# Loading the first activations through ScalarE's DMA queue instead of SyncE's in a two-layer decoder trunk

## The chip, the cores and the metric

The kernel runs on one core of a Trainium2 chip. The metric is the device time of one execution in microseconds (us). The program before was timed three times: median 2251.39 us, lowest 2250.98, highest 2251.55. A separate execution was recorded by the hardware profiler, and all durations in this document come from such recordings.

The engines are TensorE (PE, its weight loads PEld), VectorE (DVE), ScalarE (ACT), GpSimd (POOL) and SyncE (SP). SP and ACT can issue DMA transfers. Each of the two has a queue of its own, and the transfers of both run on the same 16 DMA engines. In the profile SP's queue is q1 and ACT's is q10.

## The reference

The reference is a decoder trunk of two layers for 256 tokens of width 2048, in float32.

```python
for l in range(DEPTH):                      # DEPTH = 2
    h = _rmsnorm(x, attn_norm[l])
    z = jnp.einsum('bsd,de->bse', h, w_in[l])          # 2048 -> 4934
    ...                                     # three kinds of attention on parts of z
    x = x + jnp.einsum('bsm,md->bsd', mix, w_o[l])
    h = _rmsnorm(x, ffn_norm[l])
    x = x + _conv_gated_mlp(h, ffn_w_up[l], ffn_conv_w[l], ffn_conv_b[l], ffn_w_down[l])
return _rmsnorm(x, final_norm)
```

Only the start matters here: the first RMS norm of the input x, and the first columns of the input projection w_in of layer 0.

## The kernel before, in words

All weights of both layers are laid out on the host as one stream of 128x128 blocks in the order of use. The kernel walks this stream once. A chunk is 16 blocks, a raw tile of 128x2048 float32 (1024 KB), and three raw tiles rotate (`load`, L109 to L115; the pool has bufs=3). Every chunk is converted in pieces: ACT casts it to a rounded `hi` (L140), DVE subtracts to get the rest, `lo` (L141). Five `hi` and five `lo` tiles rotate. Each product then takes matmuls with `hi` and with `lo`.

The input x arrives twice. Transposed, as eight tiles `xg` of 256 KB (two slices of 128 features each), it feeds the first norm and the first projection; in its natural layout, as two tiles `xr` of 1024 KB (L589), it is needed only for the residual much later. `Norm.split` multiplies a slice of x by the norm's gain on ACT (L396) and takes the rest on DVE (L397), giving the 16 tiles `h`. The row scale 1/rms isn't needed for these products. It is applied when a result is drained from PSUM, so its computation runs beside the first projection: eight squares of the `xg` tiles on ACT (L547), a running sum on DVE (L549), a column sum on PE (`misc`, L361), a square root on ACT with its table load (L365), a reciprocal and two scalings on DVE (L366, L369), and a second PE step that spreads the result over the rows (L376). Three PSUM banks take the first three results; the fourth block of the projection goes to the bank `s`. The next one (the tile `mm_531` in the order below) needs one of the three banks back, and that drain needs the row scale.

`load_first` (L117 to L126) issues the first three chunks in quarters of 256 KB, and between the first eight quarters the eight `xg` tiles. Before it, ACT issues the 42 columns of `par` that hold the norm's gains (21 KB) and computes one Square on a tiny tile (L277), which brings a table load. Eleven matmuls on a zeroed tile (L274) run on PE meanwhile. After `load_first` SP issues a table of constants (`cs`), the positions (`pint`) and the rest of `par`.

A scheduler orders the instructions of each engine from the program text and its own estimates; within an engine they run in that order. Each DMA signals its landing on one of eight counters, DMAHW0 to DMAHW7, which are handed out in turn; a transfer that takes a counter again waits, on the engine that issues it, until the counter's earlier transfer has landed.

Of the kernel before, what the change touches and what calls it, by code (L numbers as in the profile page):

```python
# [12 lines left out]
AF = mybir.ActivationFunctionType  # L13
# [20 lines left out]
Q_AN, Q_FN, Q_QN, Q_KN, Q_DG, Q_FB, Q_CV = 0, 16, 32, 36, 40, 41, 42  # L34
# [33 lines left out]
def kernel(ctx: ExitStack, tc: tile.TileContext, xin, xnat, pos, wstream, cst, par, fin, out):  # L68
    nc = tc.nc
# [10 lines left out]
    def nm(s):  # L80
        uid[0] += 1
        return f"{s}_{uid[0]}"

    def slot(dtype=F32):
        return slots.tile([P, 2 * T], dtype, tag="slot", name=nm("slot"))

    def tmp():
        return work.tile([P, T], F32, tag="tmp", name=nm("tmp"), bufs=15)

    def small(n):  # L90
        return work.tile([P, n], F32, tag="small", name=nm("small"), bufs=15)
# [7 lines left out]
    def f(ap):  # L99
        return ap.bitcast(F32)  # L100
# [16 lines left out]
    def load_first():  # L117
        for c in range(3):
            t = wpool.tile([P, CH * P], F32, tag="raw", name=nm("raw"), bufs=3)
            src = wflat[c * CH * P * P : (c + 1) * CH * P * P].rearrange("(p e) -> p e", p=P)  # L120
            for i in range(4):
                a = slice(i * 4 * P, (i + 1) * 4 * P)
                nc.sync.dma_start(t[:, a], src[:, a])
                if c < 2:
                    nc.sync.dma_start(xg[4 * c + i], xin[4 * c + i])
            raws[c] = t  # L126

    def convert(s, between=None):
# [135 lines left out]
    pr = [const.tile([P, Q_W], F32, tag=f"par{l}", name=f"par{l}") for l in range(DEPTH)]  # L264
# [3 lines left out]
    xg = [slot().rearrange("p (j t) -> p j t", j=2) for k in range(KT // 2)]  # L268
# [5 lines left out]
        nc.tensor.matmul(hot, heat[:, :P], heat, start=(i == 0), stop=(i == 10))  # L274
    warm = small(4)
    nc.vector.memset(warm, 0.0)
    nc.scalar.activation(warm, warm, AF.Square)  # L277
    nc.scalar.dma_start(pr[0][:, :Q_CV], par[0, :, :Q_CV])
    load_first()
    nc.sync.dma_start(cs, cst)  # L280
    nc.sync.dma_start(pint, pos)
# [284 lines left out]
    for l in range(DEPTH):  # L566
# [48 lines left out]
        for j in range(2):  # L615
            c = f(c_hi[fo, j * T : (j + 1) * T])
# [26 lines left out]
        for j in range(2):  # L643
            for h in range(H_FOX):
                if j == 0:
                    fqk.append(slot())
                i = j * H_FOX + h + 1
# [87 lines left out]
        for qo in (Q_KN, Q_QN):  # L735
            ln = Norm(q_[:, qo : qo + 4], 512)
            tiles = []
            for k in range(4):
                u = total(mm_t(hx))
                c = tmp()  # L740
# [263 lines left out]
```

## Time and profile before

| | us |
|---|---|
| median of 3 runs | 2251.39 |
| profiled execution | 2251.53 |
| its span, first to last instruction | 2249.8 |
| PE busy | 2236.4 |
| ACT busy | 1204.2 |
| DVE busy | 1487.6 |
| first weight cast on ACT starts | 5.09 |
| first matmul of the projection starts | 6.91 |

Times inside the execution count from the first instruction. The profiled execution takes 1.73 us more than its span, and 0.14 us more than the median of the runs. A row of the timeline gives start and duration, the engine, the source line, the operation, and what it writes and reads; "x2" means that two instructions are merged in it. A row of the issues gives the number of transfers, the size of one, and the median time from issue to landing.

### The profile page before, as it was taken

Reading aid. Unit: us, or ns where it says so; the run is one execution under the profiler, and the core shown is the slowest. Engines: PE = TensorE matmul, PEld = TensorE weight load, DVE = VectorE, ACT = ScalarE, POOL = GpSimd, SP = SyncE. Lnnn points to the kernel's source line nnn. Section 1 sums busy time; section 2 is a strip of 40 time slices with the busy share of each in tenths; the row PEclk is TensorE's granted clock in tenths of the full one; section 3 lists DMA queues with packets and bytes.
Section 4 is the critical chain, followed back from the end, with each engine's and each line's share of the span. In section 5 each row is a group of like instructions: output and inputs, shape, how many; then the busy total and the mean of one; then the engine's idle time right before and its main releaser. Section 6 shows DMA issues by size and latency. Waiting matters only on the chain.

```text
span 2249.8 us, 31033 instructions
## 1 busy us (share of the span) xinstructions
PE 2236.4 (99%) x12083; PEld 1929.6 (86%) x12083; DVE 1487.6 (66%) x2317; ACT 1204.2 (54%) x1867; POOL 404.7 (18%) x395
## 2 busy tenths in 40 slices
PE   9999999999999999999999999999999999999998
PEld 8888978888888888888888889788888888888886
DVE  8767766677764577775574787566666546777653
ACT  7455645555543455554454565455555435555543
POOL 4600000222210022210050110003333101222210
PEclk9999999999999999999999999999999999999999
DMA  8544445455555555555555444355555555555653
GB/s 314 200 160 159 156 141 181 162 194 194 187 206 189 186 189 187 190 202 188 187 182 193 150 167 159 131 185 178 186 185 185 207 200 187 188 187 187 208 201 114
DMA packets 60915, 413.59 MB, mean 184 GB/s; under 512 B 6880, under 2 KB 7008, under 8 KB 11744
## 3 DMA queue, kind: packets, MB, share of 16 engines
q1 hardware_dynamic: 60048, 410.54, 51.6%
q8 instruction: 95, 1.56, 0.3%
q10 hardware_dynamic: 720, 1.07, 0.1%
q14 instruction: 52, 0.43, 0.1%
HBM read 409.49 MB, written 2.10 MB: 183 GB/s over the span
## 4 chain that ended last, share of the span: by engine, by line
PE 98%; ACT 1%; DVE 0%; DMA 0%; issue 0%; DVEq 0%; SPq 0%; ACTq 0%
PE mm L195 37%; PE mm L200 19%; PE mm L249 12%; PE mm L250 12%; PE mm L251 12%; PE s L473 2%; PE mm L234 1%; PE mm L766 1%; PE mm L767 1%; PE mm L768 1%; PE pv L505 1%; PE mm L232 1%; PE s L432 0%; PE misc L376 0%; PE pv L506 0%; ACT hi L140 0%
## 5 line engine op out<-in xcount | busy, mean ns | idle before, releaser
L141 DVE TENSOR_TENSOR lo<-raw,hi 128x1024 fp32r<-128x1024 f32 (+1 forms) x776 | 974.9, 1264 | 499.4 <-ACT hi L140 461.0
L140 ACT CAST hi<-raw 128x1024 fp32r<-128x1024 f32 (+1 forms) x776 | 800.5, 1039 | 475.7 <-PE mm L251 367.1
L195 PE MATMUL mm<-h,hi 128*128 128x512 f32 x3584 | 863.8, 392 | 0.0
L195 PEld LDWEIGHTS mm<-h,hi 128*128 128x128 f32 x3584 | 664.7, 188 | 135.6 <-ACT tmp L259 1.3
L200 PEld LDWEIGHTS mm<-h,lo 128*128 128x128 f32 x3584 | 460.6, 190 | 13.6
L200 PE MATMUL mm<-h,lo 128*128 128x256 f32 x3584 | 465.4, 283 | 0.0
L249 PE MATMUL mm<-hi,slot 128*128 128x512 f32 x992 | 387.7, 391 | 0.0
L251 PE MATMUL mm<-hi,slot 128*128 128x512 f32 x992 | 384.8, 388 | 0.0
L250 PE MATMUL mm<-lo,slot 128*128 128x512 f32 x992 | 384.7, 388 | 0.0
L824 POOL TENSOR_TENSOR tmp<-tmp,rstd 128x256 f32<-128x256 f32 x176 | 193.4, 1099 | 1037.7 <-DVE tmp L261 727.7
L827 ACT ACTIVATE tmp<-tmp,par 128x256 f32<-128x256 f32 x176 | 106.0, 602 | 312.1 <-POOL tmp L824 312.1
L249 PEld LDWEIGHTS mm<-hi,slot 128*128 128x128 f32 x992 | 186.3, 188 | 41.5 <-issue 4.0
L251 PEld LDWEIGHTS mm<-hi,slot 128*128 128x128 f32 x992 | 186.2, 188 | 38.2
L250 PEld LDWEIGHTS mm<-lo,slot 128*128 128x128 f32 x992 | 186.3, 188 | 36.8
L828 DVE SCALAR_TENSOR_TENSOR tmp<-tmp,par,tmp 128x255 f32<-128x255 f32 x176 | 84.5, 480 | 150.7 <-ACT tmp L827 150.7
L259 ACT COPY tmp<-mm 128x256 f32<-128x256 f32 (+1 forms) x233 | 85.9, 369 | 62.1 <-PE mm L195 34.1
L832 POOL TENSOR_TENSOR tmp<-tmp,tmp 128x256 f32<-128x256 f32 x88 | 75.6, 859 | 211.6 <-ACT tmp L831 209.3
L261 DVE TENSOR_TENSOR tmp<-mm,tmp 128x256 f32<-128x256 f32 (+1 forms) x233 | 97.4, 418 | 5.5 <-ACT tmp L259 5.3
L829 DVE SCALAR_TENSOR_TENSOR tmp<-tmp,par,tmp 128x254 f32<-128x254 f32 x176 | 85.0, 483 | 6.2
L831 ACT ACTIVATE tmp<-tmp 128x256 f32<-128x256 f32 x88 | 36.8, 418 | 61.8 <-DVE tmp L829 61.7
L249 PE MATMUL mm<-hi,h 128*128 128x512 f32 (+1 forms) x192 | 68.3, 356 | 0.0
L251 PE MATMUL mm<-hi,h 128*128 128x512 f32 (+1 forms) x192 | 67.9, 354 | 0.0
(193 smaller groups left out, 1470.9 us busy)
## 6 DMA issues: line engine op xcount, KB each, us to landing
raw<-in_w SPq DMA_DIRECT2D x381, 1024.0 KB, 4.8
raw<-in_w SPq DMA_DIRECT2D x14, 256.0 KB, 5.3
slot<-in_x SPq DMA_DIRECT2D x8, 256.0 KB, 5.2
x<-in_xn SPq DMA_DIRECT2D x2, 1024.0 KB, 10.7
slot<-in_fin SPq DMA_DIRECT2D x4, 256.0 KB, 6.2
out<-x SPq DMA_DIRECT2D x4, 256.0 KB, 3.9
out<-x ACTq DMA_DIRECT2D x4, 256.0 KB, 4.0
par<-in_par SPq DMA_DIRECT2D x1, 325.0 KB, 7.6
```

The source lines that it names most:

```text
L140: nc.scalar.copy(hi[:, a], src[:, a])
L141: nc.vector.tensor_tensor(lo[:, a], src[:, a], f(hi[:, a]), ALU.subtract)
L195: nc.tensor.matmul(ps, ws[i][0], moving[i], start=(i == 0), stop=bool(flip and i == k - 1))
L200: nc.tensor.matmul(ps[:, :T], ws[i][1], moving[i][:, :T], start=False, stop=(not flip and i == k - 1))
L249: nc.tensor.matmul(ps[t][:, :n], s_hi, hi, start=(i == 0), stop=False)
L250: nc.tensor.matmul(ps[t][:, :n], s_hi, lo, start=False, stop=False)
L251: nc.tensor.matmul(ps[t][:, :n], s_lo, hi, start=False, stop=(i == k - 1))
L259: nc.scalar.copy(t[:rows], ps[:rows, T : 2 * T])
L261: nc.vector.tensor_tensor(u[:rows], ps[:rows, :T], t[:rows], ALU.add)
L824: nc.gpsimd.tensor_tensor(uu, u, rstd, ALU.mult)
L827: nc.scalar.activation(y, uu, AF.Identity, scale=q_[:, w + 2 : w + 3], bias=q_[:, w + 3 : w + 4])
L829: nc.vector.scalar_tensor_tensor(y[:, 2:], uu[:, : T - 2], q_[:, w : w + 1], y[:, 2:], ALU.mult, ALU.add)
```

## The change

The eight `xg` transfers are issued by ACT (`nc.scalar.dma_start`) instead of SP. The gains and the tiny Square are issued inside `load_first`, after the first `xg`. The weights stay on SP. Bytes, tiles and arithmetic are the same.

```diff
@@ -122,7 +122,10 @@
                 a = slice(i * 4 * P, (i + 1) * 4 * P)
                 nc.sync.dma_start(t[:, a], src[:, a])
                 if c < 2:
-                    nc.sync.dma_start(xg[4 * c + i], xin[4 * c + i])
+                    nc.scalar.dma_start(xg[4 * c + i], xin[4 * c + i])
+                    if c + i == 0:
+                        nc.scalar.dma_start(pr[0][:, :Q_CV], par[0, :, :Q_CV])
+                        nc.scalar.activation(warm, warm, AF.Square)
             raws[c] = t
 
     def convert(s, between=None):
@@ -274,8 +277,6 @@
         nc.tensor.matmul(hot, heat[:, :P], heat, start=(i == 0), stop=(i == 10))
     warm = small(4)
     nc.vector.memset(warm, 0.0)
-    nc.scalar.activation(warm, warm, AF.Square)
-    nc.scalar.dma_start(pr[0][:, :Q_CV], par[0, :, :Q_CV])
     load_first()
     nc.sync.dma_start(cs, cst)
     nc.sync.dma_start(pint, pos)
```

Source lines between the two edits move by 3, and lines below the second edit by 1: L140 becomes L143, L376 becomes L377. The numbers behind the names count tiles: `slot_79` to `slot_86` are the eight `xg` tiles, `raw_105` (`raw_103` in the changed kernel), `raw_114` and `raw_123` the first three chunks, `raw_247`, `raw_315` and `raw_358` the next three.

The scheduler gives ACT another beginning. Before, the first rows of ACT are these:

```order
L278 DMA par_73<-in_par 128x42
L277 ACT_TABLE_LOAD
L277 ACTIVATE small_101<-small_101 128x4 [waits DVE_49]
L140 CAST hi_149<-raw_105 128x512 [waits DMAHW1_49]
L396 ACTIVATE h_133<-slot_79,par_73 128x256 [waits DMAHW2_49,DMAHW0_49]
```

In the changed kernel:

```order
L127 DMA par_73<-in_par 128x42
L125 DMA slot_79<-in_x 128x512
L128 ACT_TABLE_LOAD
L128 ACTIVATE small_101<-small_101 128x4 [waits DVE_49]
L125 DMA slot_80<-in_x 128x512
L125 DMA slot_81<-in_x 128x512 [waits DMAHW0_49]
L125 DMA slot_82<-in_x 128x512 [waits DMAHW2_49]
L125 DMA slot_83<-in_x 128x512 [waits DMAHW4_49]
L125 DMA slot_84<-in_x 128x512 [waits DMAHW6_49]
L125 DMA slot_85<-in_x 128x512 [waits DMAHW0_49]
L125 DMA slot_86<-in_x 128x512 [waits DMAHW2_49]
L143 CAST hi_149<-raw_103 128x512 [waits DMAHW1_49]
```

All eight issues now stand ahead of the first cast, and six of them wait on a counter. By the rows of the instructions that use the tiles, counter 0 belongs in turn to `par_73`, `slot_81`, `slot_85`; counter 2 to `slot_79`, `slot_82`, `slot_86`; counter 4 to the third quarter of the first chunk and `slot_83`; counter 6 to `slot_80` and `slot_84`.

On SP, the rows behind the constants were these before:

```order
L282 DMA par_73<-in_par 128x608 [waits DMAHW7_49]
L114 DMA raw_247<-in_w 128x2048 [waits DMAHW0_49,DVE_49]
L114 DMA raw_315<-in_w 128x2048 [waits DMAHW1_49,DVE_49]
L114 DMA raw_358<-in_w 128x2048 [waits DMAHW3_49,DMAHW4_49,DMAHW2_49,DVE_49]
L587 DMA par_74<-in_par 128x650
L589 DMA x_77<-in_xn 128x2048
L589 DMA x_78<-in_xn 128x2048 [waits DMAHW5_49]
```

In the changed kernel:

```order
L283 DMA par_73<-in_par 128x608 [waits DMAHW7_49]
L588 DMA par_74<-in_par 128x650 [waits DMAHW0_49]
L590 DMA x_77<-in_xn 128x2048 [waits DMAHW1_49]
L114 DMA raw_247<-in_w 128x2048 [waits DMAHW2_49,DVE_49]
L590 DMA x_78<-in_xn 128x2048 [waits DMAHW3_49]
L114 DMA raw_315<-in_w 128x2048 [waits DMAHW4_49,DVE_49]
L114 DMA raw_358<-in_w 128x2048 [waits DMAHW5_49,DVE_49]
```

The second layer's parameters and the natural-layout x moved ahead of the fourth, fifth and sixth chunk.

On ACT, the end of the squares and what leads to the square root was this before (the rows `hi_311` and `hi_333` are the casts of `raw_247`, `rcol_381` is the square root):

```order
L547 ACTIVATE slot_304<-slot_85 128x512
L547 ACTIVATE slot_307<-slot_86 128x512
L140 CAST hi_311<-raw_247 128x1024 [waits DMAHW0_49,DVE_49,PE_49]
L140 CAST hi_333<-raw_247 128x1024 [waits DVE_49,PE_49]
L365 ACT_TABLE_LOAD [waits DMAHW5_49]
L365 ACTIVATE rcol_381<-misc_376,cs 128x2 [waits PE_49]
```

In the changed kernel `hi_311` and `hi_333` stand ahead of all eight squares, and the end of the squares is followed by this:

```order
L548 ACTIVATE slot_304<-slot_85 128x512
L548 ACTIVATE slot_307<-slot_86 128x512
L143 CAST hi_354<-raw_315 128x1024 [waits DMAHW4_49,DVE_49,PE_49]
L143 CAST hi_387<-raw_315 128x1024 [waits PE_49]
L143 CAST hi_532<-raw_358 128x1024 [waits DMAHW5_49,PE_49]
L143 CAST hi_538<-raw_358 128x1024 [waits DVE_49,PE_49]
L366 ACT_TABLE_LOAD
L366 ACTIVATE rcol_381<-misc_376,cs 128x2 [waits PE_49]
```

So the squares moved behind the casts of `raw_247`, and the square root behind the casts of two more chunks. On DVE the subtraction that makes `lo_539`, half of `raw_358`, moved between the reciprocal and the two scalings. From about the 90th instruction of ACT and DVE on, and the 120th row of PE, the order of the engines is the same as before.

## The prediction

> **What bounds the kernel now.** I read the page first: who is busy, and the chain that ended last.
>
> ```profile
> PE 2236.4 (99%) x12083; PEld 1929.6 (86%) x12083; DVE 1487.6 (66%) x2317; ACT 1204.2 (54%) x1867; POOL 404.7 (18%) x395
> PE 98%; ACT 1%; DVE 0%; DMA 0%; issue 0%; DVEq 0%; SPq 0%; ACTq 0%
> ```
>
> PE sets the time. The change touches the first microseconds only, so the question is when PE gets its work there and whether a delay could be caught up later. The busy time by stretch answers the second part (stretch and its length, then PE, PEld, DVE, ACT and POOL busy, TensorE clock, DMA share, GB/s):
>
> ```profile
> 0.00:1.45 1.45, 0.00 (x0) 0.00 (x0) 0.50 (x2) 0.28 (x1) 0.92 (x6) 1.00 0.00 0
> 1.45:6.91 5.46, 5.06 (x12) 3.47 (x12) 1.17 (x3) 2.92 (x6) 1.96 (x4) 1.00 0.80 250
> 6.91:25.27 18.36, 17.59 (x96) 15.01 (x97) 17.83 (x34) 18.34 (x36) 6.47 (x5) 1.00 1.04 400
> 25.27:32.28 7.01, 7.01 (x44) 6.26 (x45) 6.97 (x10) 4.72 (x7) 6.86 (x4) 1.00 1.02 418
> 32.28:2239.00 2206.72, 2206.72 (x11935) 1904.83 (x11933) 1457.50 (x2263) 1174.22 (x1812) 388.49 (x379) 1.00 0.51 181
> 2239.00:2249.80 10.80, 0.01 (x1) 0.00 (x0) 3.67 (x9) 3.75 (x8) 0.00 (x0) 0.69 0.52 195
> ```
>
> From 32.28 to 2239.00 PE is busy for the whole 2206.72 us, and the 10.80 us behind it hang on its last result. Nothing can absorb a delay: whatever 32.28, the start of `mm_531`, becomes, the end moves by as much. Up to 32 the DMA engines are full too (share 1.02 to 1.04 at 400 to 418 GB/s), so the order of the bytes matters. Next the timelines of PE and ACT up to there, and the last of the running sum and its scalings on DVE:
>
> ```profile
> 1.45 5.06 PE L274 MATMUL pv<-slot 128*128 128x512 f32 x11 [1.45 <-DVE small L276]
> 6.91 0.70 PE L231 MATMUL mm<-h,hi 128*128 128x512 f32 x1 [0.39 <-DVE h L397]
> 25.27 1.05 PE L361 MATMUL misc<-cs,slot 128*128 128x1 f32 x8 [0.77 <-DVE slot L549]
> 31.92 0.61 PE L376 MATMUL misc<-tmp,cs 128*128 128x128 f32 x4
> ...
> 1.17 1.28 ACT L277 ACT_TABLE_LOAD   x1 [1.17 <-PEq L993]
> 2.47 0.20 ACT L277 ACTIVATE small<-small 128x4 f32<-128x4 f32 x1
> 5.09 0.62 ACT L140 CAST hi<-raw 128x512 fp32r<-128x512 f32 x1 [2.42 <-DMA raw<-in_w]
> 19.71 2.72 ACT L547 ACTIVATE slot<-slot 128x512 f32<-128x512 f32 x5
> 22.37 2.00 ACT L140 CAST hi<-raw 128x1024 fp32r<-128x1024 f32 x2
> 24.39 1.28 ACT L365 ACT_TABLE_LOAD   x1
> 26.36 0.26 ACT L365 ACTIVATE rcol<-misc,cs 128x2 f32<-128x2 f32 x1 [0.69 <-PE misc L361]
> ...
> 25.14 2.55 DVE L141 TENSOR_TENSOR lo<-raw,hi 128x1024 fp32r<-128x1024 f32 x2
> 27.61 0.15 DVE L366 RECIPROCAL rcol<-rcol 128x2 f32<-128x2 f32 x1
> 27.80 0.50 DVE L369 TENSOR_SCALAR tmp<-cs,rcol 128x128 f32<-128x128 f32 x2
> ```
>
> PE's only waits before 32.28 are 0.39 us ahead of the first projection matmul, which follows the zero matmuls at 6.91, and 0.77 us for the sum of squares. The square root is done at 26.62, more than 5 us before PE spreads it at 31.92: that chain has slack today.
>
> **The change, part by part.** First, ACT's issues. In the changed order all eight `xg` issues stand ahead of ACT's first cast, and six wait for an earlier landing. While ACT waits there, every cast, every `h` and so all of DVE's and PE's projection work is queued behind it. Today SP does that waiting, and nobody is behind SP but transfers. The rows (issue, size, us to landing; the SP wait names what it waited for):
>
> ```profile
> par<-in_par ACTq DMA_DIRECT2D x1, 21.0 KB, 4.5
> slot<-in_x SPq DMA_DIRECT2D x1, 256.0 KB, 4.6
> SPq L125 <- DMA par<-in_par: 1.0, 1, 1.0
> 0.74 0.40 ACTq L278 DMA_DIRECT2D par<-in_par  x1
> 5.26 0.33 SPq L125 DMA_DIRECT2D slot<-in_x  x1
> q1 hardware_dynamic: 221, 0.42, 65.0%
> q10 hardware_dynamic: 128, 0.02, 5.2%
> ```
>
> `par` is issued at 0.74 and lands 4.5 us later, at 5.24; SP's own wait for that counter ended at 5.26. So `slot_81` goes out on ACT at about 5.3. The first `xg` lands today at about 5.8 (issued at 1.18, 4.6 us). In the changed kernel it shares the engines with SP's queue, which holds up to five quarters. The last two rows are the packets of both queues from 2.0 to 4.5 us, 221 against 128: with work in both, ACT's queue got between a third and a half. I take half of 400 GB/s: 256 KB (0.262 MB) then takes 1.3 us. With `par` gone at 5.24 on the slowest engine and earlier on others, the first four `xg` land near 6.2, 7.5, 8.8 and 10.1. `slot_86` waits on counter 2 for the fourth (`slot_82`); it is issued at 10.1, takes 0.4 us like `par`'s issue, and the first cast starts at **about 10.5 instead of 5.09, 5.4 later**. Lower bound: ACT's queue gets all the bandwidth and the first `xg` lands at 5.8 as now. `slot_82` is then issued at 5.8 and cannot beat the quickest landing in the kernel, that of the unhurried weight loads:
>
> ```profile
> raw<-in_w SPq DMA_DIRECT2D x381, 1024.0 KB, 4.8
> ```
>
> 4.8 less 2.6 for 1.049 MB at 400 GB/s is 2.2 us of fixed time; with 0.7 for 256 KB `slot_82` lands at 8.7, and the first cast starts at 9.1 (4.0 later). Upper bound: a third of the bandwidth, 2.0 us for each `xg`, gives 12.8 (7.7 later).
>
> The Trainium skill says in "DMA: Bandwidth & Descriptors", section "Issuing engines are not separate DMA queues", that issuing from several engines saves only the sequencer's issue time, since all queues run on the same 16 engines. By that rule the change could gain at most issue time on SP; the full engines in the stretches above agree.
>
> Second, what PE makes of that delay. Its first projection matmul moves from 6.91 to about 12.3. In the changed order three casts of the third chunk stand ahead of `h_145`, so PE waits there some 1.7 us: three subtractions of half size on DVE, 0.6 us each by the 25.14 row (two of full size in 2.55, with their overlap), less a little slack. The wait of 0.77 us for the squares sits later in PE's order now and is left out. Of the 0.77 us that PE isn't busy between 6.91 and 25.27 nothing else is left. By the delay alone `mm_531` would start at 32.28 + 5.4 + 1.7 - 0.8 = 38.6, or at 37.9 if DVE has caught up by 0.7 us at `h_145`, since its data then wait for it and not it for them; I take 37.9.
>
> Third, the bytes ahead of `raw_247`, and this decides. SP's rows today:
>
> ```profile
> 15.38 5.99 SPq L114 DMA_DIRECT2D raw<-in_w  x3
> raw<-in_w SPq DMA_DIRECT2D x1, 1024.0 KB, 6.9
> par<-in_par SPq DMA_DIRECT2D x1, 325.0 KB, 7.6
> x<-in_xn SPq DMA_DIRECT2D x2, 1024.0 KB, 10.7
> ```
>
> `raw_247` is issued at 15.38 and lands 6.9 later, at 22.28, just ahead of its cast at 22.37. In the changed order `par_74` (325 KB) and `x_77` (1024 KB) stand ahead of it: 1.38 MB at 418 GB/s is 3.3 us, and it lands at **25.6**. All other bytes ahead of it are the same, on engines that are full either way. Behind it ACT's order is a chain:
>
> - two casts of `raw_247`, 1.00 us each (22.37, 2.00, x2): 27.6
> - eight squares, 0.53 us each (five from 19.71 to 22.37): 31.9
> - four casts of `raw_315` and `raw_358`: 35.9. The chunks land 2.5 us apart at 418 GB/s, with `x_78` between: `raw_315` at 30.6, `raw_358` at 33.1, both in time, with 1.3 and 0.8 us to spare
> - table load 1.28 and square root 0.26: 37.4
>
> Then DVE: reciprocal 0.15, `lo_539` 1.2, two scalings 0.45: 39.2. Then PE's spread, 0.4 until the next matmul can start (31.92 to 32.28): `mm_531` starts at **39.7 instead of 32.28, 7.4 later**. PE itself, by the second step, would be ready at 37.9, so this chain ends last and covers the first two steps. Its cover works the other way round too: a start up to 1.8 us later than 10.5 costs nothing.
>
> Fourth, edits that cost nothing. `mm_531` also needs the PSUM drain of the first result, which stands right behind the scalings on DVE. Eight issues leave SP's queue, at 0.33 to 0.43 us each; they stood beside full DMA engines. The tiny Square stays at the start of ACT, ahead of data that isn't there. From the third chunk behind this place on, weights land earlier than PE asks (DMA share 0.51 in the long stretch).
>
> Sum, against the profiled execution: 2251.53 + 7.4 = 2258.9. The median of the runs is 0.14 lower; I keep **2258.9 us**.
>
> **The rivals.** *Only the late start counts*: `raw_247` lands earlier than 25.6, since two queues may fill the engines better, or SP reaches it sooner. For it: the start is the larger visible loss. Against it: the stretches show no idle DMA time to win. Then `mm_531` starts between 35.5 (first cast at 9.1, nothing lost at `h_145`) and 37.9: 2254.8 to 2257.2, say 2256.2.
>
> *A cold array*: the zero matmuls end at 6.51, and PE then has nothing for some 5.8 us.
>
> ```profile
> L195 PE MATMUL mm<-h,hi 128*128 128x512 f32 x3584 | 863.8, 392 | 0.0
> 7.44 0.28 PE L232 MATMUL mm<-h,lo 128*128 128x256 f32 x1
> ```
>
> The zero matmuls took 0.46 us each (5.06 for 11); the same shape later takes 0.24 (863.8 for 3584). The array began at half speed and was fast from about 7.4 on, where a half-wide matmul starts 0.53 behind the first one and takes 0.28. If PE fell back to half speed, 5.9 us of it (1.45 to about 7.4, as at the start) would lose 2.95 us, of which the wait at `h_145` swallows 1.5 and the wait for the squares the rest. Only a slow phase twice as long, losing 5.9, shows: 2.5 beyond the chain, 2261.4. For and against it this trace has nothing: no such idle stretch occurs, and the granted clock reads 1.00 in the stretch of the slow zero matmuls too. The Trainium skill, "TensorE: Matmul & The Clock Gate", section "Part 1: The HAM clock gate", says that the clock halves after an idle window of about 3.4 us and returns after a busy one; no run here shows the first half yet, and by its figure the loss would be 1.7 to 3.4 us, which is hidden.
>
> *Not slower*: the landings that ACT waits for come so early that its first cast starts before about 8.0, and `raw_247` lands before 23. Then PE starts within 3 us of today, the wait of 0.77 is gone, and the end stays within 4.5 us. If ACT's issues cost nothing at all, first cast at 5.09, it would gain up to 0.77 + 0.39: 2250.2. For it: `xg` and weights needn't stand in one line any more. Against it: two landings in a row (`slot_79`, then `slot_82`) precede the first cast in ACT's order, and the rows above show 4.5 and 4.6 us for one.
>
> **How the numbers follow.** The chain behind `raw_247`: 0.58, by itself 2257.4 to 2260.5 (0.7 us of DMA rate each way, twice). Only the late start: 0.20. Cold and long: 0.10. Not slower: 0.12. Within 0.2% means within 4.5 us of 2251.4, about what a measurement of this kernel can tell from no change. Slower takes the first, three quarters of the second and the third: 0.83; same takes the rest of the second and most of the last, 0.14; faster, which needs 2246.9, 0.03. The range reaches from the low end of the late start to the cold case: 2255.0 to 2261.6.
>
> **What would show it.** In the profile of the changed kernel ACT's first cast starts at 9 to 12 us, behind issues that wait for `par` and for `xg`; `raw_247`'s cast starts at 25 to 26, the square root at about 37, PE's spread at about 39, with PE idle before the column sum or the spread; from there on PE has no gap, and the long stretch keeps its 2206.7 us. The zero matmuls' neighbours tell the cold case: first projection matmuls 0.46 us apart instead of 0.23. I am wrong if the first cast starts before 8.5, if `raw_247` lands before 24, or if PE's stretch to the end is shorter than now.

## The result, and the profile after

The changed kernel takes 2263.74 us (median of 4 runs, 2263.52 to 2265.16) against 2251.2 us (4 runs, 2250.98 to 2251.55): a ratio of 1.0057, 95% interval 1.0045 to 1.0069. It is slower, as forecast, but by 12.5 us and not by 7.4, and the time lies above the range. The profiled execution took 2263.52 us, its span 2261.7.

The busy time by stretch, in the columns of the prediction (stretch and its length, PE, PEld, DVE, ACT and POOL busy, TensorE clock, DMA share, GB/s), cut where PE's rows cut it:

```profile
1.45:14.61 13.16, 5.07 (x12) 3.49 (x12) 1.15 (x3) 3.28 (x6) 1.95 (x4) 0.85 0.94 324
14.61:39.46 24.85, 22.38 (x116) 18.73 (x116) 23.91 (x38) 22.34 (x40) 15.35 (x12) 0.94 0.88 337
39.46:44.26 4.80, 4.80 (x24) 4.35 (x25) 3.09 (x6) 1.05 (x4) 0.00 (x0) 0.70 0.77 251
44.26:2251.00 2206.74, 2206.73 (x11934) 1904.96 (x11933) 1455.57 (x2262) 1173.93 (x1812) 380.76 (x374) 1.00 0.51 180
```

The last row is the old one: 2206.74 us from `mm_531` to the end, 2206.72 before. The whole loss lies ahead of `mm_531`, which starts at 44.26 instead of 32.28, 11.98 later. The clock column, which read 1.00 all the way to `mm_531` before, is now below it. Rows of the timelines of ACT and PE up to there:

```profile
4.53 8.24 ACTq L125 DMA_DIRECT2D slot<-in_x  x6
12.81 0.62 ACT L143 CAST hi<-raw 128x512 fp32r<-128x512 f32 x1 [9.66 <-DMA slot<-in_x]
26.53 2.00 ACT L143 CAST hi<-raw 128x1024 fp32r<-128x1024 f32 x2 [0.96 <-DMA raw<-in_w]
28.44 4.27 ACT L548 ACTIVATE slot<-slot 128x512 f32<-128x512 f32 x8
32.62 1.98 ACT L143 CAST hi<-raw 128x1024 fp32r<-128x1024 f32 x2
35.13 1.05 ACT L143 CAST hi<-raw 128x1024 fp32r<-128x1024 f32 x1 [0.54 <-DMA raw<-in_w]
37.17 1.05 ACT L143 CAST hi<-raw 128x1024 fp32r<-128x1024 f32 x1 [0.99 <-PE s L216]
40.55 0.26 ACT L366 ACTIVATE rcol<-misc,cs 128x2 f32<-128x2 f32 x1 [1.02 <-PE misc L362]
...
14.61 0.80 PE L234 MATMUL mm<-h,hi 128*128 128x512 f32 x1 [8.09 <-DVE h L398]
25.54 0.50 PE L237 MATMUL mm<-h,hi 128*128 128x512 f32 x1 [0.92 <-DVE h L398]
39.46 1.05 PE L362 MATMUL misc<-cs,slot 128*128 128x1 f32 x8 [1.51 <-DVE slot L550]
43.55 1.05 PE L377 MATMUL misc<-tmp,cs 128*128 128x128 f32 x4
```

The first cast waited 9.66 us behind ACT's own issues and started at 12.81, where 10.5 was forecast. PE waited three times: 8.09 us for the first `h`, 0.92 at `h_145`, 1.51 ahead of `misc`. Its clock, by stretch (stretch and length, PE busy, clock, DMA share, GB/s):

```profile
10.63:17.46 6.83, 2.85 (x9) 0.50 1.03 367
17.46:41.35 23.89, 21.41 (x122) 1.00 0.84 321
41.35:44.76 3.41, 3.41 (x13) 0.50 0.86 312
```

Half speed twice, for 6.83 and 3.41 us. Of these PE worked 2.85 us ahead of 17.46 and 2.91 between 41.35 and the start of `mm_531`.

**The path to `mm_531`.** The view of the chain that ended last names at each step what released it (start, length, what; parts left out):

```profile
12.82 0.62 ACT hi L143
...
26.61 0.89 DVE lo L144
27.50 1.03 ACT hi L143
28.53 3.28 ACT slot L548 x7
...
38.80 0.61 DVE slot L550
39.46 1.05 PE misc L362 x8
```

Read backwards, it leads from the column sum `misc` over the running sum on DVE, the squares on ACT and the second cast of `raw_247` to DVE's splits, and through them to ACT's first cast at 12.82. The landing of `raw_247` isn't on it, though it is close: ACT began that chunk at 26.53, after 0.96 us of waiting for the data, and the chain takes the second cast from DVE's subtraction, which ended at 27.50. Behind `misc` PE waits for nothing more. The two scalings on DVE end at 42.52, a microsecond before PE spreads their result at 43.55:

```profile
42.05 0.47 DVE L370 TENSOR_SCALAR tmp<-cs,rcol 128x128 f32<-128x128 f32 x2
```

**An account in three terms.** Between the first projection matmul and `mm_531` PE before needed 32.28 - 6.91 = 25.37 us, 0.77 of them waiting, so 24.60 of work at full clock. If nothing else counts, then `mm_531` starts at: first matmul + 24.60 + PE's waits + half of the time at half clock. For the changed kernel this is 14.61 + 24.60 + (0.92 + 1.51) + (2.85 + 2.91) / 2 = 44.52, and 44.26 was measured. So of the 11.98 us about 7.7 are the later start, 1.7 longer waits and 2.9 the clock (0.3 too much in all). This is bookkeeping: it says where PE's time went, and not yet what comes back when a cause is taken away. The experiments test that; their table stands behind them.

### The profile page after: what moved, and what is told of

Same layout as the page of the kernel before. It is cut to its first block, busy times and chain, and to the rows that moved or that the text cites. A ratio compares the mean times of both kernels' runs of the same rounds, so it can differ in the third digit from the quotient of the medians.

```text
span 2261.7 us, 31029 instructions
## 1 busy us (share of the span) xinstructions
PE 2239.0 (99%) x12083; PEld 1931.5 (85%) x12083; DVE 1487.9 (66%) x2317; ACT 1204.4 (53%) x1867; POOL 399.0 (18%) x395
## 4 chain that ended last, share of the span: by engine, by line
PE 98%; DVE 1%; DMA 0%; ACT 0%; issue 0%; SPq 0%; DVEq 0%
PE mm L198 36%; PE mm L203 19%; PE mm L252 12%; PE mm L254 12%; PE mm L253 12%; PE s L474 2%; PE mm L237 1%; PE mm L767 1%; PE mm L768 1%; PE mm L769 1%; PE pv L506 1%; PE mm L235 0%; PE s L433 0%; PE misc L377 0%; DVE lo L144 0%
## 5 line engine op out<-in xcount | busy, mean ns | idle before, releaser
L143 ACT CAST hi<-raw 128x1024 fp32r<-128x1024 f32 (+1 forms) x776 | 801.0, 1039 | 495.2 <-PE mm L254 369.0
```

Source lines behind the costliest of these rows:

```text
L143: nc.scalar.copy(hi[:, a], src[:, a])
```

## The experiments

Each kernel was timed beside runs of the kernel before on the same chip, whose medians were 2251.57, 2251.27 and 2251.27 us in the three groups (e1 to e4, e5 to e8, e9 to e12); "+" is the distance of the medians. Theory A says that the later start of ACT, passed on in full, makes the loss. Theory B is the prediction's: the chain behind `raw_247` decides and covers the start. A trace shows one execution: e9's took 2263.01 us, 1.4 more than its median, and e4's 2257.50, 1.0 more. The two longest of e3's ten executions show a mean clock of 0.997 and the others 0.998 or 0.999, so how much of the start runs at half clock seems to vary from one execution to the next.

### Fewer tiles on ACT: the dose (e3, e5)

```diff
-                    nc.scalar.dma_start(xg[4 * c + i], xin[4 * c + i])
+                    (nc.scalar if 4 * c + i < 2 else nc.sync).dma_start(xg[4 * c + i], xin[4 * c + i])
```

e5 has 4 in place of 2. In both `raw_247` is ahead of `xnat` on SP again.

> The change done for the first two x tiles alone: ACT issues those two and the gains, none of which waits; the other six stay on SP. Theory 'late start by ACT's waits': the first cast is back at about 5 us and the order of SP behind the constants is that of the kernel before; 2251.2 within 1. Theory 'sharing': the first x tile on its own queue lands near 7.1 us as in the changed kernel instead of 5.7, and the end is 1.3 later, 2252.5. Forecast's theory has nothing of its own to add here, since raw_247 stands ahead of x again. If two queues as such cost most of the 12.5 us, 2256 or more.

> Only the first four tiles of x (and the gains) are issued by ScalarE, the last four go back to SyncE; the order on SyncE is then the old one, with raw_247 ahead of the tiles of xnat. Late start by ScalarE's own waits: the third and fourth issue wait for the landings of the gains and of the first tile (4.5 and 7.1 us in the changed kernel), so the first cast starts at 7.5 to 8 us, the first projection matmul at 9.3 to 9.8, about 1.5 us behind the kernel with two tiles on ScalarE (8.02 there, mm_531 at 34.11), and the program ends at 2254.5 to 2256. Chain behind raw_247: raw_247 is ahead of xnat here as it was with two tiles, so the end is that kernel's, 2253.0 to 2254.0, whatever the start.

With two tiles, whose issues wait for nothing: 2253.52 us (2253.05 to 2256.61), +1.95. With four, of which two wait: 2256.86 us (2255.69 to 2258.33), +5.59. With all eight, six waiting, +12.5. ACT and PE of e3, then of e5:

```profile
4.45 0.62 ACT L143 CAST hi<-raw 128x512 fp32r<-128x512 f32 x1 [1.29 <-DMA raw<-in_w]
6.94 0.91 ACT L397 ACTIVATE h<-slot,par 128x256 fp32r<-128x256 f32 x2 [1.88 <-DMA slot<-in_x]
8.02 0.50 PE L234 MATMUL mm<-h,hi 128*128 128x512 f32 x1 [1.77 <-DVE h L398]
```

```profile
5.04 2.44 ACTq L125 DMA_DIRECT2D slot<-in_x  x2
7.53 0.62 ACT L143 CAST hi<-raw 128x512 fp32r<-128x512 f32 x1 [4.37 <-DMA slot<-in_x]
9.32 0.72 PE L234 MATMUL mm<-h,hi 128*128 128x512 f32 x1 [2.97 <-DVE h L398]
36.31 0.80 PE L377 MATMUL misc<-tmp,cs 128*128 128x128 f32 x4 [1.41 <-DVE tmp L370]
```

Two issues that wait (5.04, for 2.44 us) hold the first cast from 4.45 to 7.53, as expected of A. The ends don't settle A against B. e3 ended 1.0 to 1.3 us above what its first two theories gave. e5 ended 0.9 above A's range and 2.9 above B's, but B's assumed that e5's chain is e3's, and ACT's order is another one: in e5 the square root stands behind the casts of the fifth and sixth chunk, as in the changed kernel, in e3 ahead of them, as before. In e5 PE waits 1.41 us for the scalings (the last row), and the chain that ended last goes back to the landing of the fifth chunk (issued at 20.45, landed 6.77 later). So there a chain behind a weight chunk does decide. Of the 2.66 us by which `mm_531` comes later in e5 than in e3, 1.30 are the later first matmul. A second effect shows in e3. ACT waits for nothing of its own making there, yet the first `xg` lands at 6.9 and not at 5.8 as before: ACT's queue puts it beside weights that stood behind it in the old order. That this sharing is the reason is a reading; it wasn't tested apart.

### The eight tiles on GpSimd's queue (e4)

```diff
-                    nc.scalar.dma_start(xg[4 * c + i], xin[4 * c + i])
+                    nc.gpsimd.dma_start(xg[4 * c + i], xin[4 * c + i])
```

> The change with GpSimd's queue in the place of ScalarE's: the eight x tiles leave SP's queue, but no engine that computes at the start waits for their landings (ACT issues only the gains). Theory 'late start by ACT's waits': most of the 12.5 us is gone, 2251 to 2254, with the first cast near 5 us. Theory 'two queues on the same DMA engines cost': the x tiles land as late as in the changed kernel and the end stays above 2258.

2256.50 us (2255.14 to 2257.50), +4.93. The first cast starts at 4.64 and the first projection matmul at 8.03, so 7.6 of the 12.5 us come back when ACT doesn't stand behind the issues. The end is still 2.5 us above A's range (2251 to 2254). The other 5 are in the account below: the first projection matmul comes 1.1 us later than before, PE waits 2.7 us on the way, 1.0 of them for the scalings, and its clock is halved for 4.7. Here the chain that ended last does go back to the landing of the fourth chunk, `raw_247` in the changed kernel (issued at 16.67, landed 6.89 later, cast at 23.66).

### The order behind `raw_247` (e2)

```diff
             for i in range(1, DEPTH):
+                nc.vector.tensor_copy(pr[i][:, :1], rstd[:, :1])
                 nc.sync.dma_start(pr[i], par[i])
             for t in range(2):
+                nc.vector.tensor_copy(xr[t][:, :1], rstd[:, :1])
                 nc.sync.dma_start(xr[t], xnat[t])
```

The two loads wait until `rstd` is there, so the three weight chunks go first, as before the change.

> The changed kernel, but the second layer's parameters and the natural-layout x are issued only once the row scale exists (a one-column copy from it writes into their tiles first), so raw_247, raw_315 and raw_358 stand ahead of them on SP. Forecast's theory (the bytes ahead of raw_247 start the chain that sets mm_531): raw_247 lands near 23.1 instead of 26.4 and the end comes about 3 us earlier, 2260.7. Theory 'late start' (ACT's first cast at 12.8 and what follows on ACT and DVE set it): ACT only reaches the cast of raw_247 at 25.6, so at most 0.9 us less, 2262.8 to 2263.7.

2262.06 us (2261.73 to 2263.20), +10.49: 2.05 us less than the change, between B's forecast (about 3) and A's (at most 0.9). The first cast starts 0.54 us later than in the changed kernel (13.35). The casts of `raw_247` start at 26.00 without any wait for their data, only 0.53 earlier: ACT comes to them hardly sooner. The loads ahead of `raw_247` were nearly covered by the late start, and not the other way round, which speaks against B. Which path the gain came by isn't shown, since other orders changed too: `misc` stands behind five more matmuls on PE and starts later, at 40.52 instead of 39.46. By the account below the first matmul comes 0.53 us later, PE's waits are 1.38 shorter, and the time at half clock is the same.

### A warm array (e1, e8)

```diff
-    for i in range(11):
-        nc.tensor.matmul(hot, heat[:, :P], heat, start=(i == 0), stop=(i == 10))
+    for i in range(45):
+        nc.tensor.matmul(hot, heat[:, :P], heat, start=(i == 0), stop=(i == 44))
```

e1 has 42 of them.

> The changed kernel with 42 instead of 11 zero matmuls on PE, so that PE works until about 14.2 us and doesn't fall back to the slow clock before its first projection matmul at 14.6; the order of all engines is otherwise that of the changed kernel (2263.7 us). Theory 'the first slow stretch is hidden' (PE waits at h_145 anyway): 2263.7 within 0.5, and the wait at h_145 grows from 0.9 us to about 2.4. Theory 'the cold array costs its own loss': about 1.5 us less, 2262.2, and the wait at h_145 stays 0.9.

> The changed kernel with 45 zero matmuls ahead instead of 11, a number at which the orders of ScalarE and VectorE up to mm_531 are the changed kernel's own. The clock stays at 1.0 from the start to the wait ahead of misc. If the first stretch at half clock is hidden behind the casts and splits: misc still at 39.3 to 39.6 and the end 2263.0 to 2264.2; if the second stretch (41.35 to 44.76) also goes, 2262.0 to 2262.6. If that first stretch is paid in full (6.83 us at half clock, 3.4 us): 2260.0 to 2260.8.

e1 took 2266.58 us (2265.57 to 2267.39), +15.0. It can't be read as meant, because with 42 matmuls the scheduler put a weight cast on ACT ahead of the copy that drains the first bank, and PE met a new wait of 2.28 us for that drain, ahead of `mm_531` (46.73).

With 45 the order of ACT and DVE is the changed kernel's up to there. e8: 2262.83 us (2262.59 to 2262.96), +11.56, 1.0 us less than the change. The clock was expected to stay full up to `misc`. Its column does read 1.00 until 26.28, but PE stands 1.77 us ahead of `h_145` (0.92 in the changed kernel) and runs at half clock from 26.28 to 29.70. A faster PE waits longer for the same `h`, and here a slow stretch begins 0.39 us behind that wait. `h_145` comes 10.94 us after the first projection matmul, in the changed kernel 10.93. The first slow stretch taken alone was thus covered by DVE, as the prediction said; the clock as a whole wasn't.

### GpSimd beside DVE (e6, e7, e12)

In the changed kernel twelve small scalings on GpSimd run beside DVE's late splits and the running sum; in the kernel before they run from 18.80 to 38.63. Held back until `rstd` is there (e6: the changed kernel, e7: the kernel before):

```diff
         one = tmp()
-        v.memset(one, 1.0)
+        v.tensor_scalar(one, rstd, 0.0, 1.0, ALU.mult, ALU.add)
```

> The changed kernel, with GpSimd's scalings of b_r made to wait until rstd is there, so that they no longer run beside VectorE from 19.6 to 35.4 us. The result is the same in value. VectorE slowed by GpSimd: the subtractions of 128x512 come back from 0.72 to 0.61 us and those of h from 0.47 to 0.36, the wait at h_145 (0.92 us) goes, the wait ahead of misc (1.51 us) shrinks to 0.8 or less, the second stretch at half clock (41.35 to 44.76) may go with it; mm_531 at 40.5 to 43, the end at 2260 to 2262.5. Rival, VectorE is slow for a reason of its own: durations and end stay, 2263.5 to 2264.2. If the copies of kr that queue behind the late scalings become a wait of the array, the end is above 2264.2 and a new wait stands behind 60 us.

> The kernel before, with the same late scalings on GpSimd. If VectorE beside GpSimd costs something on the path before: the adds of the squares finish earlier and mm_531 starts 0.2 to 0.8 us ahead of 32.28, the end is 2250.4 to 2251.0. If the chain before does not hang on VectorE there: 2251.0 to 2251.8, no difference.

e6: 2260.72 us (2260.25 to 2260.89), +9.45, so 3.1 us of the change's loss go. GpSimd's scalings in the changed kernel, then the durations on DVE beside them (min/median/max in ns, first and last start) of the half-size subtractions and the running sum:

```profile
19.63 15.79 POOL L565 TENSOR_SCALAR b_r<-tmp,cs 6x256 fp32r<-6x256 f32 x12 [16.12 <-DMA cs<-in_cst]
```

```profile
L144 DVE TENSOR_TENSOR lo<-raw,hi x8: 679/780/881, 19.0 to 26.6; 128x512 fp32r<-128x512 f32 x8
L550 DVE TENSOR_TENSOR slot<-slot,slot x7: 683/882/886, 30.7 to 38.7; 128x512 f32<-128x512 f32 x7
```

and in e6 without them:

```profile
L144 DVE TENSOR_TENSOR lo<-raw,hi x8: 678/678/681, 19.4 to 26.0; 128x512 fp32r<-128x512 f32 x8
L550 DVE TENSOR_TENSOR slot<-slot,slot x7: 682/692/694, 30.4 to 37.7; 128x512 f32<-128x512 f32 x7
```

Each costs 0.1 to 0.2 us more beside GpSimd. Without that PE no longer waits at `h_145`, waits 1.16 instead of 1.51 at `misc` (0.8 or less was expected), and has no second slow stretch. The Trainium skill says in "SBUF — State Buffer", section "Who interferes with whom", that a DVE instruction with two SBUF inputs contends with a GpSimd instruction that reads SBUF. These rows agree. The same section calls the shared port pair an exclusive lock; here a scaling takes about 1.3 us (15.79 for twelve) and the adds beside it grew by 0.2, so a lock held for a whole scaling doesn't show in them.

e7 gains nothing and ends above both of its ranges: 2253.26 us (2252.79 to 2254.92), +1.99. `mm_531` starts 0.86 us earlier, at 31.42, but PE waits twice further on (1.27 and 0.65 us), where it had no wait before. The scalings and the first of the waits:

```profile
33.96 13.66 POOL L564 TENSOR_SCALAR b_r<-tmp,cs 6x256 fp32r<-6x256 f32 x12
49.89 1.22 PE L200 MATMUL mm<-h,lo 128*128 128x256 f32 x8 [1.27 <-DVE lo L141]
```

The scalings are over at 47.62, so these waits aren't theirs directly. DVE's order is another one there, with other small instructions between its subtractions, and the two subtractions that PE waits for take 1.4 us instead of 1.23 beside GpSimd's copies, which come later too. What share each has is open.

e12 replaces the scalings in the kernel before by two copies that write the same values:

```diff
-            for h in range(H_FOX):
-                v.tensor_scalar(b_r[o : o + 6, h], one[o : o + 6], cs[o : o + 6, C_SEL + h : C_SEL + h + 1], None, ALU.mult)
+            v.tensor_copy(b_r[o : o + 6], cs[o : o + 6, C_SEL : C_SEL + H_FOX].unsqueeze(2).to_broadcast([6, H_FOX, T]))
```

> The kernel before, with GpSimd's twelve scalings of a tile of ones by the columns of the selector replaced by two copies of the selector, broadcast along the row; the values in b_r are the same. VectorE is then next to undisturbed both at 19 to 39 us and later: misc starts 0.5 to 1 us ahead of 25.27, no new wait at 50 us as with the late scalings, the end 2250.2 to 2251.0. If the scalings beside VectorE cost nothing on the path: 2251.0 to 2251.6.

A clear miss: 2255.78 us (2253.77 to 2257.57), +4.51. Its timeline on GpSimd and PE, and the durations of the running sum:

```profile
18.91 5.98 POOL L563 CAST b_r<-cs 6x1536 fp32r<-6x1536 f32 x2 [16.55 <-DMA cs<-in_cst]
27.12 1.05 PE L361 MATMUL misc<-cs,slot 128*128 128x1 f32 x8 [2.55 <-DVE slot L549]
```

```profile
L549 DVE TENSOR_TENSOR slot<-slot,slot x6: 689/712/1770, 19.2 to 26.4; 128x512 f32<-128x512 f32 x6
```

Two adds of the running sum, at 21.80 and 23.67, took 1.77 us each instead of 0.7 while the long copies ran, PE waited 2.55 us ahead of `misc`, and a slow stretch of 3.41 us followed. Two copies of 3 us each thus held DVE up more than the short scalings did. No version tried here beats the kernel before.

### Two and three edits together (e9, e10, e11)

The changed kernel with the late scalings of e6, and with it the 45 matmuls of e8 (e9), the order of e2 (e10), or both (e11).

> The changed kernel with both edits: 45 zero matmuls ahead instead of 11, and GpSimd's scalings of b_r held back until rstd is there. TensorE's account (later start, plus longer waits, plus half of the time it runs at half clock before mm_531): first projection matmul at 14.9 to 15.1 (+8.1), no half clock up to mm_531, waits of 1.2 to 2.6 us at misc and h_145 together against 0.8 before; mm_531 at 40.8 to 42.2, the end at 2259.6 to 2261.2. If the chain on ScalarE and VectorE alone sets misc, warmth only lengthens the wait there and the end is that of the late scalings alone, 2260.4 to 2261.0. If the clock costs nothing once the waits are equal, there is nothing to gain and the end is 2260.7 or later.

> The changed kernel with the late scalings, and with par_74 and xnat held back behind rstd so that raw_247, raw_315 and raw_358 stand ahead of them on SyncE (the old order). Chain behind raw_247: the casts of raw_247 start 1 us earlier than with the late scalings alone (27.07), the wait at misc (1.16 us) goes to 0.4 or less, the end is 2259.2 to 2260.2. Late start decides: the end stays at 2260.3 to 2261.2, since ScalarE comes to those casts no earlier than 25.9.

> All three edits on the changed kernel: 45 zero matmuls, late scalings, raw_247 and its followers ahead of xnat on SyncE. What is left of the change is then the late start by ScalarE's own issues alone: first projection matmul 8.0 to 8.2 us behind the kernel before, mm_531 at 40.2 to 41.0 and the end at 2258.8 to 2260.0. If some further cost of the change is at work, not less than 2260.5; if the late start is partly absorbed, below 2258.5.

e9: 2261.59 us (2260.70 to 2263.01), +10.3; e10: 2259.87 us (2259.18 to 2260.52), +8.6; e11: 2259.78 us (2259.63 to 2260.06), +8.5. e9 gained nothing on e6 and missed the range forecast for it by the account: the warm PE waited 1.01 us at `h_145` and 1.55 ahead of `misc`, and a slow stretch followed from 40.00 to 43.41. In its trace the chain that ended last goes back to the landing of `raw_247` (issued at 18.58, landed 8.44 later). e10 is 0.85 us better than e6 and came out as B had it, not A: the casts of `raw_247` start at 26.02 instead of 27.07, PE has no wait left, and the end lies in B's range. So once the scalings are out of the way, the order on SP, with the orders that change with it, is worth about 1 us. e11 ended in the range forecast for it; the late start is nearly all that is left in it. Its timeline on PE, and the stretch up to `mm_531` (columns as in the first fence):

```profile
14.78 0.50 PE L234 MATMUL mm<-h,hi 128*128 128x512 f32 x1
24.96 0.50 PE L237 MATMUL mm<-h,hi 128*128 128x512 f32 x1 [1.01 <-DVE h L398]
40.77 3.92 PE L198 MATMUL mm<-h,hi 128*128 128x512 f32 x16
```

```profile
14.70:40.77 26.07, 24.93 (x141) 21.13 (x141) 24.96 (x44) 23.07 (x43) 0.00 (x0) 1.00 0.74 271
```

No stretch at half clock, no scalings on GpSimd, the old order on SP, one wait of 1.01 us: `mm_531` at 40.77, 8.49 later than before, of which 7.87 are the later first matmul (14.78 instead of 6.91). That is about what the issues on ACT cost by themselves. It isn't exact: e11 has the late scalings and the kernel before hasn't, and there they brought `mm_531` 0.86 us forward (e7).

### The account over all kernels

In us, each from its own trace; "sum" is first matmul + 24.60 + waits + half of the half-clock time up to `mm_531`.

| kernel | first matmul | PE's waits | at half clock | sum | `mm_531` measured | end |
|---|---|---|---|---|---|---|
| before | 6.91 | 0.77 | 0 | 32.28 | 32.28 | 0 |
| changed | 14.61 | 2.43 | 5.76 | 44.52 | 44.26 | +12.5 |
| e1, 42 zero matmuls | 14.58 | 5.21 | 3.41 | 46.10 | 46.73 | +15.0 |
| e2, old order on SP | 15.14 | 1.05 | 5.73 | 43.66 | 43.05 | +10.5 |
| e3, two on ACT | 8.02 | 0.45 | 3.41 | 34.78 | 34.11 | +2.0 |
| e4, on GpSimd | 8.03 | 2.73 | 4.72 | 37.72 | 37.41 | +4.9 |
| e5, four on ACT | 9.32 | 1.67 | 3.44 | 37.31 | 36.77 | +5.6 |
| e6, late scalings | 14.94 | 1.16 | 3.26 | 42.33 | 41.90 | +9.5 |
| e7, before with late scalings | 6.60 | 0.42 | 0 | 31.62 | 31.42 | +2.0 |
| e8, 45 zero matmuls | 14.95 | 2.46 | 3.41 | 43.72 | 43.76 | +11.6 |
| e9, e6 and e8 | 14.72 | 2.72 | 3.41 | 43.75 | 43.96 | +10.3 |
| e10, e6 and e2 | 14.89 | 0 | 4.93 | 41.96 | 40.89 | +8.6 |
| e11, all three | 14.78 | 1.01 | 0 | 40.39 | 40.77 | +8.5 |
| e12, before with two copies | 6.80 | 2.55 | 3.41 | 35.66 | 35.61 | +4.5 |

In thirteen rows of fourteen the sum is within 0.7 us; in e10 it is 1.07 too high, and why is open. In all seven rows with a slow stretch near the first matmul (changed, e2 to e6, e10) the sum is too high, by 0.3 to 1.1, so half of that time is probably too dear a price. The waits aren't independent of the other terms (e8, e9), so a term taken out doesn't come back in full. In e1, e4, e5, e7 and e12 the part behind `mm_531`, 2217.5 us before, is 0.8 to 2.1 us longer; half clock or new waits of PE fall there too.

## Why the prediction was wrong

**What bounds the kernel** held. Nothing behind `mm_531` absorbs anything: the long stretch is the same to 0.02 us. That each of the edits held to be free costs nothing wasn't tested apart.

**First step, ACT's start.** The mechanism was right: issues in ACT's order that wait for landings, and everything queued behind them. Mis-sized is the landing of the first four `xg`, forecast at 6.2, 7.5, 8.8 and 10.1. ACT's issues in the changed kernel, five rows of the timeline:

```profile
1.18 0.45 ACTq L125 DMA_DIRECT2D slot<-in_x  x1
4.53 0.34 ACTq L125 DMA_DIRECT2D slot<-in_x  x1
7.08 0.33 ACTq L125 DMA_DIRECT2D slot<-in_x  x1
8.04 1.02 ACTq L125 DMA_DIRECT2D slot<-in_x  x2
10.67 0.33 ACTq L125 DMA_DIRECT2D slot<-in_x  x1
```

The time to landing of those at 1.18 and 4.53, from the view of the issues:

```profile
slot<-in_x ACTq DMA_DIRECT2D x1, 256.0 KB, 5.9
slot<-in_x ACTq DMA_DIRECT2D x1, 256.0 KB, 6.1
```

And packets, MB and share of both queues, from 7.0 to 8.5 us:

```profile
q1 hardware_dynamic: 274, 0.50, 86.8%
q10 hardware_dynamic: 59, 0.10, 18.1%
```

`slot_79` landed at 7.1 (1.18 + 5.9), `slot_80` at 8.7 (1.72 + 7.0), `slot_81` at 10.6 (4.53 + 6.1). The issue at 8.04 is that of `slot_83`, which had waited for the third quarter of the first chunk. `slot_82` could be issued only at 7.08, when `slot_79` was in, and landed near 12.4, where the last of ACT's issues waited for it. I reckoned by bandwidth, with a queue that always has work. The share itself was about right: from 4.5 to 7.0 us, with work in both, ACT's queue moved 0.40 MB and SP's 0.43. (The row that it was read from counted packets; in bytes it was 0.02 against 0.42 MB.) But the waits emptied the queue: from 7.0 to 8.5 us it moved 0.10 MB beside SP's 0.50. What counted was two landings in a row at 5 to 6 us each. The upper bound of this step, 12.8, is what came, but it was reckoned from a third of the bandwidth and not from landings, so that it fits is luck.

**Second step, PE.** The first projection matmul came at 14.61 instead of 12.3, all of it the first step's miss. The wait at `h_145` was foreseen and was 0.92 us, not 1.7; the wait ahead of `misc`, left out there, was 1.51.

**Third step, the deciding chain: here the prediction failed.** It said of the chain behind `raw_247` that "this chain ends last and covers the first two steps", so that a start 1.8 us later would cost nothing. (Its steps add up to 39.6; the 39.7 is a tenth too much.) The casts of `raw_247` started at 26.53 (25.6 forecast), held by their data for 0.96 us, and the squares ended at 32.7 (31.9): so far within 0.9. Then the four casts ended at 38.2 instead of 35.9, and the root at 40.8 instead of 37.4, behind 0.54 us for the landing of `raw_358`, 0.99 for PE to free a `hi` tile and 1.02 for `misc`. Up to the root the chain was reckoned as if only ACT were on it. Its links hang on PE and DVE, which the late start had delayed; so it couldn't cover that start. Nor did it end last: the trace leads from `mm_531` over `misc` and DVE to the first cast and not to the landing of `raw_247`, and the scalings were done a microsecond before PE came to them. Still, the two paths ended close together, and in other versions (e4, e5, e9) a chain behind a weight chunk did end last. Taking the reorder on SP back gave 2.05 us (e2) and 0.85 (e10). What it was to hide came to 8.5 (e11).

**The rival of the cold array** gave the closest time, 2261.4, at a chance of 0.10, still 2.3 us too low. It priced one slow stretch and found most of it hidden; e8 agrees with that for the first one. Not foreseen was a second, from 41.35, behind a wait of only 1.51 us. The Trainium skill, "TensorE: Matmul & The Clock Gate", section "Part 1: The HAM clock gate", gives about 3.4 us for its window; the trace agrees, with slow stretches of 3.41 and 6.83. Its rule of one idle window doesn't cover the second stretch, which follows on 1.51 us of waiting and 1.05 us of one-column matmuls.

**Not seen at all**: GpSimd. The row at 25.14, from which DVE's durations were taken, stood beside the scalings itself, and what they cost was never asked. In the changed kernel it was some 3 us by e6, part of which came through the clock; in the kernel before it was 0.86 us at `mm_531` (e7).

**Of the signs named beforehand**, the first cast (9 to 12), the root (37) and PE's spread (39, came at 43.55) came later than said; the cast of `raw_247` (25 to 26) by half a microsecond; PE's stretch without a gap and the idle time ahead of the column sum were right. None of the three signs of being wrong came (`raw_247` landed at 26.5, not before 24), so they didn't test the step that failed. The rival "only the late start" had most of the mechanism, though not its condition, an earlier `raw_247`: its price was that of the first step's upper bound, with the waits and the clock on top.

## What to carry to other kernels

Before a transfer is moved to a computing engine's queue, look for the issues that must wait for a counter there, and count the landings that follow one another: six waiting issues made two landings in a row here, of 5 to 6 us each, which stand ahead of that engine's own work, and a queue that waits runs dry. Where two delays end close together, don't let one "cover" the other until it is clear that the cover doesn't hang on the same engines: the changed kernel's chain did, and e11 kept 8.5 of 12.5 us. A delay also moves work beside other work and to other clock stretches, so durations read from the kernel before may not hold.

## What the hardware did that I had not expected

- TensorE went to half clock for 3.41 us after waits far shorter than that: 1.51 us and eight one-column matmuls (the changed kernel), 1.77 us (e8), 2.55 us and the same matmuls (e12). A wait of 1.05 or 1.16 us with the same matmuls behind it had no such stretch (e2, e6). The edges of the slow stretches in the changed kernel (10.63, 17.46, 41.35 and 44.76) lie 2, 7 and 1 times 3.41 us apart, so where a wait falls between such marks may count beside its length; no run varied that.
- Small GpSimd instructions on 6 partitions made DVE's subtractions and adds on 128 partitions 15 and 27% longer (0.678 to 0.780 us, 0.692 to 0.882), and the two long copies of e12 made two adds 1.1 us longer.
- Not the hardware but the scheduler: 42 zero matmuls ahead of everything (45 did not) changed ACT's order some 40 us later, and e1 lost 2.28 us by it.
